# Reordering and rebalancing the convolution branch of a two-layer hybrid encoder on one NeuronCore

## The chip, the cores and the metric

The kernel runs on 1 core of a Trainium2 chip, in one launch. The metric is device microseconds of that core; the time given is the median of three runs. Beside them one execution was taken with the hardware profiler; all views below are of that execution.

## The reference

The input is 512 tokens by 1024 features, float32. Two layers follow one another; each adds half a SwiGLU feed-forward block, then a mixer, then half of a second SwiGLU block, with an RMS norm ahead of each part and one at the end. In the mixer the normed input is projected by `w_in` to 1696 columns: 384 for query latents, 256 for key/value latents, 32 for a rotary key, and 2 x 512 for a convolution branch.

```python
def conv_group(u_raw, conv_w, conv_b, ln_g, ln_b):
    a, g = u_raw[..., :CONV_W], u_raw[..., CONV_W:]
    u = a * jax.nn.sigmoid(g)
    y = lax.conv_general_dilated(u, conv_w[:, None, :], window_strides=(1,),
        padding=[(CONV_K - 1, 0)], feature_group_count=CONV_W, ...)
    y = y + conv_b
    return jax.nn.silu(layer_norm(y, ln_g, ln_b))
...
x = x + 0.5 * swiglu(rms_norm(x, ffn1_norm[l]), ...)
p = rms_norm(x, mix_norm[l]) @ w_in[l]
attn = mla_group(...)          # 8 heads, block-causal, RMS-normed q and k, rotary part
conv = conv_group(p[..., o_cv:], ...)
x = x + jnp.concatenate([attn, conv], axis=-1) @ w_out[l]
x = x + 0.5 * swiglu(rms_norm(x, ffn2_norm[l]), ...)
x = rms_norm(x, post_norm[l])
```

The depthwise convolution is causal and has 31 taps on each of 512 channels.

## The kernel before

Activations lie transposed, 128 features by 512 tokens a tile. Every float32 matrix product is made of three passes in the reduced format (`mm3`, lines 153 to 155): high part times high part, high times low, low times high. So every weight needs a high part, cast by ACT (L137), and a remainder, source minus high part. The remainder is made in one of three ways by `load_w`: a subtraction on DVE, one on POOL (kind "wo"; both L143), or, for kind "sum", ACT writes the negated source rounded to the reduced format (L140) and POOL issues a DMA that adds the source from HBM onto it (L141). High parts and remainders have four buffers each, raw weights three; SyncE issues the raw loads.

The program is written with a tile framework. It knows the data dependencies, and at build time it fixes the order of instructions on each engine by simulating the program with a planner's costs: of what is ready, what comes first in the program goes first. `tc.issue_after(ins)` lets instructions of the block go on their engine only behind `ins`. On the chip each engine then executes its instructions in that order.

The mixer (`mix_body`, once a layer) takes its projections in the order of `SEQ`: query latents, the first two convolution groups, key latents (`latent_k`), their transposes (`kt`, L714), token terms, queries (`uq`), keys (`uk`), and convolution inputs 2 and 3 (`conv_in`). The four convolution groups are 128 channels each; `glu` leaves group c's input in `u[c]`. Then come the eight heads, staged by hand: transposes, scores, softmax, transposed probabilities, values and, for each pair of heads, a split of the output (`turn_out`). The attention output is in `at`.

The convolution stands behind attention in the program, so its instructions fill gaps of the engines while attention runs. `TAPS` gives for each group how many of the 31 taps (the last tap, with the bias, among them) do not go to DVE. Tap products s = 1 to n-1 are made by ACT into one of three buffers `pr` (L931) and added by POOL into `ys[c]` (L933). The other taps are fused multiply-adds on DVE into a PSUM bank `acc` (L927), which ACT begins (L923). Group 2 has all its taps on ACT and POOL, group 3 has all on DVE. POOL's adds of s >= 16, and those of groups past 1, stand behind the last reciprocal root of the keys. A DVE add joins the two parts (L938); three more DVE adds form the sum of the four groups, `ysum` (L941).

The layer norm over 512 channels follows: a matmul with a constant matrix gives the mean (`pm`, L952), DVE subtracts it (L958), ACT squares, DVE adds the squares, PE sums them (L197), POOL takes the reciprocal root (L172), PE spreads it (L216), and scale and SiLU finish each group (L968, L970). Meanwhile PE runs early groups: for output tile m the half of `w_out` that multiplies attention (12 matmuls). `E1`, `E2`, `E3` and `WOG` say how many of them stand ahead of the mean, of the sums, of the spread and of the rest; output tiles are then finished in groups of `WOG`. The temporaries `tmp()` have five buffers that are shared by all of this.

Of the kernel before, what the change touches and what calls it, by code (L numbers as in the profile page):

```python
# [7 lines left out]
FP = mybir.dt.float32  # L8
# [3 lines left out]
AF = mybir.ActivationFunctionType  # L12
ALU = mybir.AluOpType
AX = mybir.AxisListType

P = 128
D = 1024
S = 512
L = 2
KD = D // P  # L20
# [3 lines left out]
DR = 32  # L24
# [3 lines left out]
KVL = 256  # L28
# [5 lines left out]
WC = 1024  # L34
# [3 lines left out]
NP = 3  # L38
NC = 2
CHUNKS = ((0, 2), (2, 5), (5, 8), (8, 11))  # L40
TAPS = (14, 17, 31, 0)
AHEAD = 2
PAUSE = 16
SEQ = "q0 R c1 q1 q2 qo k kt tt uq uk c2 c3"
# [2 lines left out]
GLUP = 0  # L47
EARLY = "s"
PRELOAD = 1
E1 = 0  # L50
E2 = 2
E3 = 3
WOG = 3
WAKE = 10
KS = (0, 2, 4, 6, 1, 3, 5, 7)
WOP = 4
# [17 lines left out]
def encoder_kernel(ctx: ExitStack, tc: tile.TileContext, xT, consts, vecs, rgain, wgu1, wd1, wdq1,  # L74
# [11 lines left out]
    def nm(s):  # L86
        uid[0] += 1
        return f"{s}{uid[0]}"
# [4 lines left out]
    def tmp(w=S, dt=FP):  # L93
        return tmps.tile([P, w], dt, tag="t", name=nm("t"))

    def bank():
        return psum.tile([P, S], FP, tag="ps", name=nm("ps"))

    def tiny(tag, w, dt=FP):
        return small.tile([P, w], dt, tag=tag, name=nm(tag))  # L100

    V, A, G, T = nc.vector, nc.scalar, nc.gpsimd, nc.tensor
# [26 lines left out]
    def vv(l, name):  # L129
        o, w = VOFF[name]  # L130
        return vec[:, l, o:o + w]

    def load_w(src, w, kind=""):
        raw = wpool.tile([P, WC], FP, tag="raw", name=nm("raw"), bufs=3)
        nc.sync.dma_start(out=raw[:, :w], in_=src)
        hi = wpool.tile([P, WC], FR, tag="wh", name=nm("wh"))
        order["cast"] = A.copy(hi[:, :w], raw[:, :w]).ins  # L137
        lo = low()
        if kind == "sum":
            A.activation(lo[:, :w], raw[:, :w], AF.Copy, scale=-1.0)  # L140
            G.dma_start(out=lo[:, :w], in_=src, accum_op=ALU.add)  # L141
            return hi, lo
        (G if kind in POOLW.split() else V).tensor_tensor(lo[:, :w], raw[:, :w], hi[:, :w].bitcast(FP),  # L143
                                                          ALU.subtract)
        return hi, lo

    def low():
        return wpool.tile([P, WC], FR, tag="wl", name=nm("wl"))

    order = {}  # L150

    def mm3(o, lh, ll, rh, rl, first, last, free=False):
        T.matmul(o, lh, rh, start=first, stop=False, skip_group_check=free)  # L153
        T.matmul(o, lh, rl, start=False, stop=False, skip_group_check=free)  # L154
        order["mm"] = T.matmul(o, ll, rh, start=False, stop=last, skip_group_check=free).ins  # L155
        return order["mm"]
# [52 lines left out]
    def spread(r):  # L209

        dg = tmp()
        V.tensor_tensor(dg.rearrange("p (t j) -> p t j", t=NT),
                        ident[:, None, :].to_broadcast([P, NT, P]),
                        r[:, :, None].to_broadcast([P, NT, P]), ALU.mult)
        ps = bank()
        order["spread"] = T.matmul(ps, ones, dg, start=True, stop=True).ins  # L216
        return ps
# [7 lines left out]
    def group(o, w, rhs, ks, n, ts=slice(0, S)):  # L225

        for k in ks:
            c = slice(k * P, (k + 1) * P)
            order["product"] = mm3(o, w[0][:, c], w[1][:, c], rhs[k][0][:, ts], rhs[k][1][:, ts], k == 0, k == n - 1)
# [386 lines left out]
    def mix_body(kpool, l, gx, norm, done):  # L616
        u, order = [], {}

        def kept(dt=FP):
            return kpool.tile([P, S], dt, tag="m", name=nm("m"), bufs=10)  # L620
        ys = [kpool.tile([P, S], FP, tag="y", name=nm("y"), bufs=3) if n else None for n in TAPS]

        def glu(pa, pg):
            tg = tmp()
            V.tensor_tensor(tg, pg, R, ALU.mult)
            sg = tmp()
            order["gate"] = A.activation(sg, tg, AF.Sigmoid).ins
            ta = tmp()
            V.tensor_tensor(ta, pa, R, ALU.mult)
            uc = kept()  # L630
            (G if GLUP else V).tensor_tensor(uc, ta, sg, ALU.mult)
            u.append(uc)

        def conv_in(c):
            pp = []
            for j in range(2):
                ps = bank()
                group(ps, load_w(wcv[l, 2 * c + j], WC, f"c{c}"), gx, range(KD), KD)
                pp.append(ps)
            glu(*pp)  # L640

        gql, gkl = vv(l, "gql"), vv(l, "gkl")
        KW = KVL + DR
        stq = Stats()
        cqT, ckT, pq, scqs, vs = [], [], [], [], []
        ssl, sspe = tiny("ssl", NT), tiny("sspe", NT)
# [18 lines left out]
        def latent_k():  # L665

            pk = [bank() for _ in range(NT)]
            for k0 in range(0, KD, 3):
                n = min(3, KD - k0)
                wh, wl = load_w(wkl[l, :, k0 * KW:(k0 + n) * KW], n * KW, "k")  # L670
                for k in range(k0, k0 + n):
                    cs = slice((k - k0) * KW, (k - k0 + 1) * KW)
                    for t in range(NT):
                        ts_ = slice(t * P, (t + 1) * P)
                        mm3(pk[t][:, :KW], gx[k][0][:, ts_], gx[k][1][:, ts_], wh[:, cs], wl[:, cs],
                            k == 0, k == KD - 1)
            for t in range(NT):
                A.copy(ckl[t // 2][:, t % 2], pk[t][:, :KVL])
                A.copy(cke[:, t], pk[t][:, KVL:KW])
                j = tmp()  # L680
                A.activation(j[:, :KVL], pk[t][:, :KVL], AF.Square, accum_out=ssl[:, t:t + 1])
                j = tmp()
                A.activation(j[:, :DR], pk[t][:, KVL:KW], AF.Square, accum_out=sspe[:, t:t + 1])


        tabs = []
# [73 lines left out]
        def up_kv(w, t, n=S):  # L760

            ts_ = slice(t * P, (t + 1) * P)
            ps = bank()
            for k in range(2):
                cs = slice(k * n, (k + 1) * n)
                mm3(ps, ckT[k][0][:, ts_], ckT[k][1][:, ts_], w[0][:, cs], w[1][:, cs], k == 0, k == 1)
            return ps
# [127 lines left out]
        with tc.issue_after(order["turned"]):  # L895
            for t in range(NT):
                ps = up_kv(wv, t)
# [15 lines left out]
        ysum = None  # L913
        for c, n in enumerate(TAPS):
            tap = lambda k: cw[:, c * CK + k:c * CK + k + 1]
            acc = psum.tile([P, S], FP, tag="cv", name=nm("cv"), bufs=1) if n < CK else None
            first = dict(func=AF.Identity, scale=tap(CK - 1), bias=cb[:, c:c + 1])
            if n:
                A.activation(ys[c], u[c], **first)
            for s in range(n or 1, CK):  # L920
                k = CK - 1 - s
                if s == n:
                    A.activation(acc[:, s:], u[c][:, :S - s], AF.Copy, scale=tap(k))  # L923
                    continue
                if s == 1 and not n:
                    A.activation(acc, u[c], **first)
                V.scalar_tensor_tensor(acc[:, s:], u[c][:, :S - s], tap(k), acc[:, s:], ALU.mult, ALU.add)  # L927
            for s in range(1, n):
                k = CK - 1 - s
                pr = kpool.tile([P, S], FP, tag="pr", name=nm("pr"), bufs=3)  # L930
                A.activation(pr[:, s:], u[c][:, :S - s], AF.Copy, scale=tap(k))  # L931
                with tc.issue_after(order["keys"]) if s >= PAUSE or c > 1 else nullcontext():
                    order["conv"] = G.tensor_tensor(ys[c][:, s:], ys[c][:, s:], pr[:, s:], ALU.add).ins  # L933
            if not n:
                A.copy(u[c], acc)
                ys[c] = u[c]
            elif n < CK:
                V.tensor_tensor(ys[c][:, n:], ys[c][:, n:], acc[:, n:], ALU.add)  # L938
            if c:
                last, ysum = ysum or ys[0], ysum or tmp()  # L940
                V.tensor_tensor(ysum, last, ys[c] if n else acc, ALU.add)  # L941
        early = []

        def early_groups(ms):
            with tc.issue_after(heads[H - 1][EARLY]):
                for m in ms:
                    early.append(bank())
                    group(early[m], wo[m], at, range(4), KD)

        early_groups(range(E1))  # L950
        pm = bank()
        T.matmul(pm, onesm, ysum, start=True, stop=True)  # L952
        if PRELOAD:
            A.activation(tiny("pre", 1), ysum[:, 0:1], AF.Silu)
        early_groups(range(E1, E2))
        st = Stats()
# [5 lines left out]
        pr = spread(r)  # L962
        early_groups(range(E3, WOG))
        lg, lb = vv(l, "lg"), vv(l, "lb")
        cv = []
        for c in range(4):
            z = tmp()
            V.tensor_tensor(z, ys[c], pr, ALU.mult)  # L968
            s = tmp()
# [3 lines left out]
        ac = at + cv  # L973
        for m0 in range(0, KD, WOG):
            ms = range(m0, min(m0 + WOG, KD))
            os = [bank() for _ in ms] if m0 else early
# [77 lines left out]
    gx = []  # L1054
    st = Stats()
    f = gained(0, "g1", gx, first_gain)
# [20 lines left out]
    gx = [gx[KS.index(m)] for m in range(KD)]  # L1077
# [27 lines left out]
    for l in range(L):  # L1105
        nx, st1, done = follow(l, "gm")
        ffn(l, gx, norm, wgu1, wd1, wdq1, vv(l, "g1"), done, w0 if l == 0 else None)
        gx = nx
        nx, st2, done = follow(l, "g2")
        mix(l, gx, Norm(st1), done)  # L1110
        gx = nx
# [3 lines left out]
        if l + 1 < L:  # L1115
# [10 lines left out]
            gx = nx  # L1126
# [118 lines left out]
```

## Time and profile before

| what | value |
|---|---|
| median of 3 runs | 1814.83 us (1812.89 to 1814.99) |
| profiled execution, its own time | 1811.83 us |
| its span, first to last instruction | 1810.0 us |
| mean granted TensorE clock | 0.994 |
| PE / DVE / ACT / POOL busy | 1777.9 / 1502.8 / 1099.6 / 411.9 us |

Times of views are in microseconds from the span's start. A row of a timeline gives start, length, engine, line, operation, the tiles written and read, shape, count, and in brackets how long the engine had stood idle before it and what ended that. A row of the waits gives the total, the number of times and the longest. A row for one source line gives least, median and greatest length in nanoseconds. Buffer numbers are left out of names, so that `t` is any temporary and `ps` any PSUM bank. A matmul's length overlaps with the next one's; the spacing of starts is the pace.

### The profile page before, as it was taken

What the parts mean: (1) busy time and instruction counts of PE and PEld (TensorE: products, weight loads), DVE (VectorE), ACT (ScalarE), POOL (GpSimd) and SP (SyncE); (2) the same over time, 40 slices, a digit from 0 to 9 for tenths busy, and PEclk for the clock granted to TensorE, in tenths of its full rate; (3) what the DMA queues carried; (4) which work ended last, traced back from release to release, by engine and by line L of the source; (5) the groups of instructions that cost most, each with busy time, mean ns of one, the idle gap of its engine ahead of it and who ended that gap; (6) DMA issues with size and microseconds to landing.
All of it is one profiled execution on the core that took longest, in us unless ns stands there. A gap on an engine that the chain in (4) does not pass through costs nothing. (4 is left out here: it accounts for less than half of the span.)

```text
span 1810.0 us, 29098 instructions
## 1 busy us (share of the span) xinstructions
PE 1777.9 (98%) x11238; PEld 1585.2 (88%) x11238; DVE 1502.8 (83%) x2271; ACT 1099.6 (61%) x1729; POOL 411.9 (23%) x335
## 2 busy tenths in 40 slices
PE   9999999999999999999999999999999999999998
PEld 7899999888668899999888999998886788999997
DVE  7898988679956989898779989876899669989884
ACT  5565656477953575756645657554778535656564
POOL 1000000278714000000320000002876320000102
PEclk9999999999999999999999999999999999999999
DMA  4657574324203466665426575743250126575642
GB/s 169 174 124 184 130 186 112 108 84 118 51 12 111 117 161 160 154 162 135 122 65 169 121 193 119 194 112 110 80 130 23 37 86 169 132 180 135 178 120 73
DMA packets 70411, 226.14 MB, mean 125 GB/s; under 512 B 7936, under 2 KB 8320, under 8 KB 70272
## 3 DMA queue, kind: packets, MB, share of 16 engines
q1 hardware_dynamic: 54000, 169.74, 29.5%
q0 software_dynamic: 16128, 54.53, 17.6%
q8 instruction: 88, 1.44, 0.3%
q14 instruction: 51, 0.42, 0.1%
q10 hardware_dynamic: 144, 0.00, 0.0%
HBM read 222.15 MB, written 2.10 MB: 124 GB/s over the span
## 5 line engine op out<-in xcount | busy, mean ns | idle before, releaser
L154 PE MATMUL ps<-r,wh 128*128 128x256 f32 (+1 forms) x2556 | 812.5, 318 | 0.0
L153 PE MATMUL ps<-r,wh 128*128 128x256 f32 (+1 forms) x2556 | 809.2, 320 | 2.3 <-ACT wh L1064 1.3
L155 PE MATMUL ps<-r,wl 128*128 128x256 f32 (+1 forms) x2364 | 756.7, 322 | 1.8 <-DVE wl L245 1.6
L153 PEld LDWEIGHTS ps<-r,wh 128*128 128x128 f32 x2556 | 483.8, 189 | 45.0 <-ACT wh L137 3.4
L154 PEld LDWEIGHTS ps<-r,wh 128*128 128x128 f32 x2556 | 484.6, 190 | 34.9 <-issue 1.4
L155 PEld LDWEIGHTS ps<-r,wl 128*128 128x128 f32 x2364 | 448.3, 190 | 37.8 <-DVE wl L245 3.4
L372 PE MATMUL ps<-xj,wh 128*128 128x512 f32 x864 | 304.8, 392 | 4.6 <-DVE t L425 4.6
L137 ACT CAST wh<-raw 128x1024 fp32r<-128x1024 f32 (+3 forms) x148 | 130.8, 891 | 190.7 <-PE ps L154 93.1
L389 POOL DMA_DIRECT2D ls<-in_wgu x72 | 62.5, 869 | 734.3 <-ACT ls L388 604.7
L243 ACT CAST wh<-fr 128x1024 fp32r<-128x1024 f32 (+1 forms) x160 | 157.8, 986 | 111.3 <-DVE fr L409 47.8
L143 DVE TENSOR_TENSOR wl<-raw,wh 128x1024 fp32r<-128x1024 f32 (+3 forms) x132 | 147.0, 1122 | 84.1 <-ACT wh L137 83.5
L245 DVE TENSOR_TENSOR wl<-fr,wh 128x1024 fp32r<-128x1024 f32 (+1 forms) x160 | 182.3, 1139 | 20.5 <-ACT wh L243 20.5
L372 PEld LDWEIGHTS ps<-xj,wh 128*128 128x128 f32 x864 | 161.3, 188 | 36.3 <-DVE t L425 6.3
L933 POOL TENSOR_TENSOR y<-y,pr 128x511 f32<-128x511 f32 (+29 forms) x118 | 160.9, 1368 | 32.6 <-ACT pr L931 26.4
L373 PE MATMUL ps<-xj,ls 128*128 128x256 f32 x576 | 161.3, 280 | 0.0
L245 DVE TENSOR_TENSOR wl<-raw,wh 128x1024 fp32r<-128x1024 f32 (+1 forms) x100 | 113.5, 1136 | 14.8 <-ACT wh L243 14.3
L243 ACT CAST wh<-raw 128x1024 fp32r<-128x1024 f32 (+1 forms) x100 | 98.1, 981 | 44.8 <-PE ps L154 27.7
L190 POOL TENSOR_TENSOR r<-r,t 128x512 f32<-128x512 f32 x45 | 76.5, 1709 | 175.6 <-ACT t L186 174.8
L373 PEld LDWEIGHTS ps<-xj,ls 128*128 128x128 f32 x576 | 108.3, 188 | 0.2
L388 ACT ACTIVATE ls<-fr 128x1024 fp32r<-128x1024 f32 (+1 forms) x56 | 56.1, 1001 | 85.6 <-PE ps L373 49.6
L931 ACT ACTIVATE pr<-m,vec 128x511 f32<-128x511 f32 (+29 forms) x118 | 85.7, 738 | 15.4 <-POOL y L933 15.0
L927 DVE SCALAR_TENSOR_TENSOR cv<-m,vec,cv 128x493 f32<-128x493 f32 (+29 forms) x118 | 85.8, 727 | 4.2 <-ACT cv L923 2.9
(243 smaller groups left out, 2869.2 us busy)
## 6 DMA issues: line engine op xcount, KB each, us to landing
fr<-in_wgu SPq DMA_DIRECT2D x112, 512.0 KB, 4.1
ls<-in_wgu POOLq DMA_DIRECT2D x72, 512.0 KB, 5.9
raw<-in_wgu SPq DMA_DIRECT2D x62, 512.0 KB, 5.1
fr<-in_wdq SPq DMA_DIRECT2D x48, 384.0 KB, 5.4
ls<-in_wdq POOLq DMA_DIRECT2D x32, 384.0 KB, 4.7
raw<-in_wd SPq DMA_DIRECT2D x32, 384.0 KB, 3.1
raw<-in_wd SPq DMA_DIRECT2D x32, 256.0 KB, 2.7
raw<-in_wcv SPq DMA_DIRECT2D x16, 512.0 KB, 3.6
```

The costliest lines, as they stand in the source:

```text
L137: order["cast"] = A.copy(hi[:, :w], raw[:, :w]).ins
L143: (G if kind in POOLW.split() else V).tensor_tensor(lo[:, :w], raw[:, :w], hi[:, :w].bitcast(FP), ALU.subtract)
L153: T.matmul(o, lh, rh, start=first, stop=False, skip_group_check=free)
L154: T.matmul(o, lh, rl, start=False, stop=False, skip_group_check=free)
L155: order["mm"] = T.matmul(o, ll, rh, start=False, stop=last, skip_group_check=free).ins
L243: A.copy(hi[:, :w], src[:, :w])
L245: order["lo"] = V.tensor_tensor(lo[:, :w], src[:, :w], hi[:, :w].bitcast(FP), ALU.subtract).ins
L372: T.matmul(o, w[0][:, c], both, start=start and k == 0, stop=False, skip_group_check=True)
L373: last = T.matmul(o[:, 0:HS], w[1][:, c], both[:, 0:HS], start=False, stop=k == 3, skip_group_check=True).ins
L927: V.scalar_tensor_tensor(acc[:, s:], u[c][:, :S - s], tap(k), acc[:, s:], ALU.mult, ALU.add)
L931: A.activation(pr[:, s:], u[c][:, :S - s], AF.Copy, scale=tap(k))
L933: order["conv"] = G.tensor_tensor(ys[c][:, s:], ys[c][:, s:], pr[:, s:], ALU.add).ins
```

## The change

It makes five edits, all in the mixer and so once a layer.

1. ACT's products s >= 5 of groups 1, 2 and 3 stand, in ACT's order, behind the last square of the key latents (`order["latent"]`, L683).
2. Group 3 gets five taps off DVE: one starting activation on ACT, four products on ACT with four adds on POOL, and a joining add on DVE. The DVE taps go from 30 to 25. Tiles of tag `y` are now taken group by group; group 3 takes the buffer that group 0 leaves, because group 0's joined result now goes into `u[0]` (its first 14 columns by an ACT copy).
3. `ysum` is kept in `u[1]`, the input of group 1, in place of a temporary.
4. The four weight tiles of convolution inputs 2 and 3 are loaded as kind "sum": the remainder leaves DVE for an ACT copy and a POOL-issued DMA.
5. `E1` goes from 0 to 1 and `WOG` from 3 to 4: one early group stands ahead of the mean, one of four behind the spread, and output tiles are finished in two groups of four.

```diff
-TAPS = (14, 17, 31, 0)
+TAPS = (14, 17, 31, 5)
+HELD = 5
...
-E1 = 0
+E1 = 1
 E2 = 2
 E3 = 3
-WOG = 3
+WOG = 4
...
-        ys = [kpool.tile([P, S], FP, tag="y", name=nm("y"), bufs=3) if n else None for n in TAPS]
+        ys = []
...
-                group(ps, load_w(wcv[l, 2 * c + j], WC, f"c{c}"), gx, range(KD), KD)
+                group(ps, load_w(wcv[l, 2 * c + j], WC, "sum" if c > 1 else "c1"), gx, range(KD), KD)
...
-                A.activation(j[:, :DR], pk[t][:, KVL:KW], AF.Square, accum_out=sspe[:, t:t + 1])
+                order["latent"] = A.activation(j[:, :DR], pk[t][:, KVL:KW], AF.Square,
+                                               accum_out=sspe[:, t:t + 1]).ins
...
+            ys.append(kpool.tile([P, S], FP, tag="y", name=nm("y"), bufs=3) if n else None)
...
-                A.activation(pr[:, s:], u[c][:, :S - s], AF.Copy, scale=tap(k))
+                with tc.issue_after(order["latent"]) if c and s >= HELD else nullcontext():
+                    A.activation(pr[:, s:], u[c][:, :S - s], AF.Copy, scale=tap(k))
...
-                V.tensor_tensor(ys[c][:, n:], ys[c][:, n:], acc[:, n:], ALU.add)
+                y = ys[c]
+                if c == 0:
+                    ys[c] = u[c]
+                    A.copy(ys[c][:, :n], y[:, :n])
+                V.tensor_tensor(ys[c][:, n:], y[:, n:], acc[:, n:], ALU.add)
             if c:
-                last, ysum = ysum or ys[0], ysum or tmp()
+                last, ysum = ysum or ys[0], u[1]
                 V.tensor_tensor(ysum, last, ys[c] if n else acc, ALU.add)
```

## The prediction

> **What bounds the kernel now.** I read the page first, then what PE waits for, then a table of stretches through the first mixer (L0, about 320 to 560 us) with the matching stretches of the second (L1).
>
> ```profile
> span 1810.0 us, 29098 instructions
> PE 1777.9 (98%) x11238; PEld 1585.2 (88%) x11238; DVE 1502.8 (83%) x2271; ACT 1099.6 (61%) x1729; POOL 411.9 (23%) x335
> PE ps L952 <- DVE t L941: 6.9, 2, 3.5
> PE ps L714 <- ACT r L678: 4.3, 2, 2.2
> 401.60:403.70 2.10, 0.00 (x0) 0.00 (x0) 1.90 (x3) 2.10 (x6) 2.02 (x2) 1.00 0.08 33
> 403.70:410.50 6.80, 6.79 (x26) 6.70 (x27) 6.73 (x15) 6.80 (x30) 6.00 (x7) 0.51 0.27 77
> 426.70:448.50 21.80, 21.80 (x98) 17.98 (x97) 21.80 (x38) 11.79 (x17) 18.65 (x16) 1.00 0.59 166
> 456.70:508.40 51.70, 50.16 (x353) 33.09 (x352) 48.31 (x95) 43.86 (x111) 30.91 (x25) 1.00 0.11 26
> 511.90:516.50 4.60, 4.60 (x12) 3.34 (x13) 3.38 (x6) 2.60 (x5) 0.00 (x0) 0.63 0.00 0
> 1301.40:1308.20 6.80, 6.80 (x26) 6.70 (x27) 6.73 (x15) 6.80 (x30) 5.92 (x6) 0.51 0.28 80
> 1409.20:1425.00 15.80, 15.62 (x67) 12.00 (x68) 8.98 (x15) 6.44 (x11) 1.03 (x1) 1.00 0.00 1
> ```
>
> In a stretch's row stand its length, then the busy time of PE, weight loads, DVE, ACT and POOL, then the granted clock. PE is busy 98% of the span, and the change removes no matmul, so only two things can be won: the 32 us in which PE stands idle, and stretches where it runs at a low clock. The two longest waits are both in the mixer, once a layer. The first, on the key-latent copies (L678), is followed in both layers by 6.8 us at clock 0.51. The second, on the group sums (L941), is followed in L0 by 4.6 us at 0.63 and in L1 by none. Between them PE is full (21.80 of 21.80) or nearly so (50.16 of 51.70), though DVE is nearly full too.
>
> **The latent copies held first.**
>
> ```profile
> 398.22 0.71 ACT L931 ACTIVATE pr<-m,vec 128x507 f32<-128x507 f32 x1
> 401.34 0.72 ACT L931 ACTIVATE pr<-m,vec 128x506 f32<-128x506 f32 x1 [2.41 <-POOL y L933]
> 401.96 0.82 ACT L137 CAST wh<-raw 128x768 fp32r<-128x768 f32 x1
> 402.68 0.71 ACT L931 ACTIVATE pr<-m,vec 128x505 f32<-128x505 f32 x1
> 403.30 0.35 ACT L678 COPY r<-ps 128x256 f32<-128x256 f32 x1
> 401.27 0.29 PE L155 MATMUL ps<-wh,r 128*128 128x288 f32 x1
> 403.71 0.62 PE L714 MATMUL ps<-cst,r 128*128 128x128 f32 x2 [2.14 <-ACT r L678]
> 450.23 0.32 PE L815 MATMUL ps<-cst,kn 128*96 128x128 f32 x1 [0.83 <-DVE kn L784]
> ```
>
> PE ends the key latents at 401.56, but ACT stands 2.41 us before product s=6 of group 1, which waits for POOL to free one of three product buffers; the cast and s=7 follow, and only then the copy. ACT executes in order, so the copy pays for POOL. Products s=5, 6 and 7 of group 1 are those now put behind the last latent square. ACT is then free from 398.9, the cast can go there, and the first copy costs about 0.35 plus a hand-over: I leave 0.45 us of the wait. Won per layer: 1.7 of idle, and (1 - 0.51) x 6.8 = 3.3 of lost clock if the gap is then too short to lower it; after the 0.83 us gap at 450 the clock stayed at 1.00 (stretch from 456.70). Both layers: 10.0 us. Bounds: 0, if another wait as long takes its place, to 4.3 + 6.7 = 11.0. Behind the held products queue only POOL's adds of group 1, costed below.
>
> **The end of attention.**
>
> ```profile
> 506.50 1.89 PE L876 MATMUL ps<-r,m 128*64 128x512 f32 x14
> 511.86 0.70 PE L952 MATMUL ps<-t,onesm 128*128 128x512 f32 x1 [3.46 <-DVE t L941]
> 508.52 0.69 DVE L879 TENSOR_TENSOR t<-ps,t 128x512 f32<-128x512 f32 x1 [1.65 <-PE ps L876]
> 509.12 0.68 DVE L941 TENSOR_TENSOR t<-y,y 128x512 f32<-128x512 f32 x1
> 511.12 0.68 DVE L941 TENSOR_TENSOR t<-t,cv 128x512 f32<-128x512 f32 x1
> 1409.23 1.12 PE L952 MATMUL ps<-t,onesm 128*128 128x512 f32 x2 [3.46 <-DVE t L941]
> 1423.31 1.19 PE L153 MATMUL ps<-r,wh 128*128 128x512 f32 x4
> 482.09 9.43 POOL L933 TENSOR_TENSOR y<-y,pr 128x488 f32<-128x488 f32 x7 [0.44 <-ACT pr L931]
> 427.39 0.39 PE L154 MATMUL ps<-r,wh 128*128 128x512 f32 x1
> 427.62 0.39 PE L155 MATMUL ps<-r,wl 128*128 128x512 f32 x1
> ```
>
> POOL's last group add ends at 491.5, yet the first of the three sums starts at 509.12, right behind the last reader of attention's temporaries (L879), after DVE stood idle 1.65 us. I read that as a wait for one of the five temporaries, not for data. In the freed u[1] the sums need none. The mean (L952) can then start when PE leaves the last values at 508.4, or after the nine matmuls of early group 0 whose operands exist, 9 x 0.23 = 2.1 us later (0.23 is the spacing of the two rows at 427). From the mean to the first convolution product L1 took 1423.31 - 1409.23 = 14.1 us, with PE busy nearly throughout; early groups 0 to 3 are that work, and they ran before too, so a fourth early group by itself adds nothing. Won per layer: 3.46 with the mean at once, 1.4 with it 2.1 later; I take 2.8, as the mean may also slip in earlier. L0 gets (1 - 0.63) x 4.6 = 1.7 more, for its clock. Both: 7.3; bounds 2.8 to 8.6.
>
> **Taps, remainders and queues.**
>
> ```profile
> L927 DVE SCALAR_TENSOR_TENSOR cv<-m,vec,cv x118: 685/728/755, 373.2 to 1398.1; 128x494 f32<-128x494 f32 x6, 128x493 f32<-128x493 f32 x6, 128x492 f32<-128x492 f32 x6, 128x491 f32<-128x491 f32 x6
> L931 ACT ACTIVATE pr<-m,vec x118: 700/722/852, 373.1 to 1386.1; 128x511 f32<-128x511 f32 x6, 128x510 f32<-128x510 f32 x6, 128x509 f32<-128x509 f32 x6, 128x508 f32<-128x508 f32 x6
> L933 POOL TENSOR_TENSOR y<-y,pr x118: 1207/1268/2105, 373.9 to 1387.7; 128x511 f32<-128x511 f32 x6, 128x510 f32<-128x510 f32 x6, 128x509 f32<-128x509 f32 x6, 128x508 f32<-128x508 f32 x6
> L938 DVE TENSOR_TENSOR y<-y,cv x4: 656/666/675, 396.9 to 1344.1; 128x498 f32<-128x498 f32 x2, 128x495 f32<-128x495 f32 x2
> 425.52 2.35 DVE L143 TENSOR_TENSOR wl<-raw,wh 128x1024 fp32r<-128x1024 f32 x2
> L140 ACT ACTIVATE wl<-raw x8: 1042/1052/1059, 438.5 to 1354.4; 128x1024 fp32r<-128x1024 f32 x8
> L141 POOL DMA_DIRECT2D wl<-in_wout x8: 870/890/1147, 444.3 to 1355.7; - x8
> DMA to landing us min/median/max: 5.1/6.4/8.7
> 420.62 2.00 ACT L137 CAST wh<-raw 128x1024 fp32r<-128x1024 f32 x2
> ```
>
> Per layer DVE loses five taps, 5 x 0.73 = 3.6, gains one add of 0.67, and loses four remainders of 1.18, 4.7: 7.7 less. ACT gains 4 x 0.72 of products and 4 x 1.05 of negated copies, 7.1 in all; its 14-column copy is small, and the other starting activations replace two of the old form. POOL gains 4 x 1.27 of adds and 4 x 0.89 of issues, 8.6. On POOL they push the last add from 491.5 to about 500, plus up to 5 for the hold; the sums are wanted at 508.4, so this is hidden. Without that cover each us past 508 is a us of PE. ACT's four products come after group 2's and lie where ACT stood idle behind 490.
>
> PE gets from the lighter DVE at most the 0.83 at the keys (L0 alone) and the 1.54 us a layer that it idles inside attention, 3.9 in all; below, 0. I take 1.8, since most of those gaps inside attention end at ACT.
>
> The new path of a remainder is on PE's path. Queries free the buffer for group 2's first weights at 420.6; the cast ends at 421.6, the negated copy at 422.65 at best, and only then POOL issues. With the median landing of 6.4 the remainder is there at 429.05; PE uses it at 427.62. With a 0.4 hand-over PE waits 1.8 us per layer, 3.6 in all. DVE's subtraction was done in time. Best: landing 5.1 and no hand-over, 0.1 a layer; worst: an add of 1.27 ahead and 8.7, 5.0 a layer. The other three have 5.5 us of PE work (24 matmuls) more each, so I put them at 0.
> [...]
>
> Output groups in fours want their last two weights about 5 us earlier, prepared by POOL: 0.5 a layer, 1.0 in all, bounds 0 to 4, by the two early matmul groups (5.5) that hid them.
>
> Sum: -10.0 - 7.3 - 1.8 + 3.6 + 1.0 = -14.5 us. The profiled execution took 1811.83 (span 1810.0 and 1.83 around it), 3.00 under the median of 1814.83. So 1797.3 for a like execution, 1800.3 for the median. All best: -11.0 - 8.6 - 3.9 + 0.2 = -23.3, 1791.5.
>
> **Rivals.** *The remainder's path becomes the new stall (slower).* If the first remainder of group 2 waits behind POOL's adds and reciprocal roots and lands late, PE idles over 2 us there and, as behind the latents, loses 3.3 more to the clock. The gains make 19.1 us for both layers, less 1.0: the point is a wait of 18.1 / 2 - 3.3 = 5.8 us a layer. At 8 us it costs 2 x 11.3 = 22.6 against 18.1: +4.5, 1819. For it: POOL is 18.65 of 21.80 busy there and DVE 21.80; against: the worst of my bounds is 5.0.
> [...] The eight issues of 0.87 to 1.15 us show no long one, though none ran at the queries.
>
> *The tail gains little.* The order on each engine is fixed at build time; if early group 0, complete with its last operand, stands before the mean, the mean starts near 511 as now, PE idles behind the four groups instead, and the end of attention gives 2.8 or less: with a landing wait of 3 (and its clock in one layer) -14.5 + 4.5 + 2.4 + 3.3 = -4.3, 1810.5.
>
> *The hold does nothing.* PE may wait at the same place for the cast or for another copy: -14.5 + 10.0 = -4.5, and with a landing wait of 3 a layer -2.1, 1812.7.
>
> **How the numbers follow.** A difference of 0.2%, 3.6 us, is about what measurement can tell from none. Forecast 0.56, tail 0.16, hold 0.08, remainder stall 0.20. The likeliest gives 1800.3, its own range 1792 to 1808. Faster takes the forecast and the tail, 0.72; same 0.08; slower 0.20. The range runs from 1791 to 1817, which leaves out the worse half of the slow rival and little below.
>
> **What would show it.** Right: the wait of L714 on L678 under 0.6 us and clock 1.00 behind it; L941 well ahead of the last L879; L952 within 2.5 us of the last L876; a wait of PE on the remainder's landing of 1 to 3 us once a layer; POOL's last group add before the last values. Wrong: a gap over 2 us before group 2's products with a low clock behind it, or L952 still waiting over 3 us.

## The result and the profile after

The changed kernel takes 1825.34 us (median of 4 runs, 1824.19 to 1825.70) against 1814.91 for the kernel before: 1.0058 times as long, interval 1.0041 to 1.0075. The forecast was 1800.3. The profiled execution took 1825.7 us, with a span of 1823.9. In the code after, lines lie a little further down: the transfer of a remainder is issued at L142, the reciprocal root is L173, a product L935, a POOL add L937, the mean L960.

The page and the waits of PE after:

```profile
PE 1779.7 (98%) x11238; PEld 1581.8 (87%) x11238; DVE 1500.1 (82%) x2255; ACT 1116.4 (61%) x1751; POOL 425.3 (23%) x351
PE ps L156 <- DMA wl<-in_wcv: 17.3, 2, 9.0
PE ps L835 <- ACT r L841: 4.5, 7, 1.1
PE ps L154 <- ACT r L161: 2.8, 2, 1.4
PE ps L154 <- ACT wh L138: 2.1, 3, 1.0
```

Both waits that the prediction wanted gone are gone: neither the key-latent copies nor the group sums are in the list. In their place stands a larger one, 17.3 us in two waits, for the remainder of convolution input 2.

To see where the time went I cut each mixer at four matmuls: the last of the key latents, the first of the scores, the last set of row sums, the first convolution product. The rows are the first mixer's stretches from latents to the last query and from there to the scores, before and then after (length, busy PE, weight loads, DVE, ACT, POOL, clock):

```profile
401.30:421.10 19.80, 17.66 (x91) 17.27 (x90) 19.32 (x36) 18.58 (x53) 18.49 (x17) 0.83 0.21 61
421.10:456.70 35.60, 34.77 (x162) 28.80 (x161) 35.21 (x57) 25.56 (x38) 31.25 (x24) 1.00 0.60 157
456.70:505.20 48.50, 46.96 (x323) 31.21 (x322) 47.14 (x93) 42.33 (x109) 30.91 (x25) 1.00 0.12 27
```

```profile
401.60:416.00 14.40, 14.40 (x91) 14.24 (x90) 14.13 (x28) 11.59 (x38) 9.71 (x11) 1.00 0.28 87
416.00:462.80 46.80, 36.82 (x163) 29.66 (x162) 40.66 (x61) 33.73 (x52) 39.90 (x33) 0.89 0.70 166
462.80:513.30 50.50, 47.05 (x323) 31.18 (x321) 46.28 (x90) 48.57 (x118) 38.20 (x31) 1.00 0.12 25
```

The hold did what it was to do: 14.40 us in place of 19.80, PE full, clock 1.00. The next stretch then grew by 11.2 us, with 10 us of PE idle. The third row is attention, 2 us longer, with ACT busy 48.57 of 50.50 where it had been 42.33 of 48.50. The table gives both layers of all kernels, from the starts of those matmuls.

| kernel | median us | latents to scores | scores to last row sums | to first convolution product |
|---|---|---|---|---|
| before | 1814.9 | 55.5 / 54.4 | 48.4 / 49.1 | 22.4 / 20.8 |
| after | 1825.3 | 61.1 / 61.5 | 50.5 / 50.8 | 20.0 / 20.0 |
| after, remainders on DVE (e1) | 1825.4 | 58.2 / 60.3 | 53.0 / 52.7 | 20.0 / 20.0 |
| remainders alone (e2) | 1825.5 | 61.4 / 61.5 | 48.5 / 48.5 | 22.8 / 22.4 |
| after, first remainder on DVE (e3) | 1828.5 | 62.2 / 57.0 | 53.9 / 52.8 | 20.0 / 20.0 |
| hold alone (e4) | 1824.0 | 56.7 / 60.3 | 49.6 / 48.2 | 22.4 / 20.8 |
| after, issue first (e6) | 1810.7 | 51.8 / 53.1 | 50.6 / 50.1 | 22.0 / 22.6 |
| four product buffers (e7) | 1825.1 | 59.9 / 59.6 | 48.5 / 48.5 | 22.4 / 22.4 |
| hold, fewer taps (e8) | 1819.1 | 55.2 / 59.7 | 49.6 / 48.2 | 22.4 / 22.1 |
| sums alone (e9) | 1812.0 | 54.4 / 54.4 | 50.4 / 49.2 | 21.7 / 22.2 |
| hold, adds behind keys (e11) | 1813.1 | 50.5 / 50.1 | 50.8 / 50.8 | 24.6 / 24.6 |
| the same with remainders (e12) | 1805.8 | 51.1 / 49.9 | 50.2 / 49.3 | 23.2 / 22.9 |
| hold, remainders, issue first (e13) | 1811.0 | 51.3 / 53.5 | 50.2 / 49.9 | 20.8 / 22.4 |
| after, adds behind keys (e14) | 1805.8 | 49.4 / 51.2 | 50.6 / 50.0 | 20.5 / 22.1 |
| e12, fewer adds (e15) | 1843.3 | 51.3 / 49.4 | 48.4 / 47.5 | 43.1 / 43.1 |
| remainders, adds behind keys (e16) | 1813.9 | 56.5 / 54.5 | 49.3 / 49.3 | 24.0 / 21.3 |

Where PE loses it, in the timelines of PE, ACT and POOL after:

```profile
423.85 0.40 PE L155 MATMUL ps<-r,wh 128*128 128x512 f32 x1
433.20 0.80 PE L156 MATMUL ps<-r,wl 128*128 128x512 f32 x1 [8.95 <-DMA wl<-in_wcv]
433.80 0.63 PE L154 MATMUL ps<-r,wh 128*128 128x512 f32 x1
418.53 1.14 ACT L141 ACTIVATE wl<-raw 128x1024 fp32r<-128x1024 f32 x1
407.42 0.60 POOL L692 TENSOR_TENSOR tab<-cst,rg 128x64 f32<-128x64 f32 x2 [4.37 <-DVE wkl L727]
417.96 3.31 POOL L937 TENSOR_TENSOR y<-y,pr 128x503 f32<-128x503 f32 x2
421.77 1.65 POOL L173 TENSOR_TENSOR scq<-ssh,minus_half 128x8 f32<-128x8 f32 x1 [0.51 <-DVE ssh L751]
423.39 1.26 POOL L937 TENSOR_TENSOR y<-y,pr 128x501 f32<-128x501 f32 x1
424.59 0.90 POOL L142 DMA_DIRECT2D wl<-in_wcv  x1
DMA to landing us min/median/max: 5.5/8.0/11.1
```

ACT had the negated copy ready at 419.67. POOL issued the transfer only at 424.59: ahead of it in POOL's order stood two held adds, a root that itself had to wait, and one more add. It landed when PE started, 433.2. The row at 407.42 shows the other side: POOL now idles 4.37 us right behind the latents, where before it was busy with six adds of group 1, four of which are now held:

```profile
400.03 8.57 POOL L933 TENSOR_TENSOR y<-y,pr 128x509 f32<-128x509 f32 x6
409.16 0.60 POOL L690 TENSOR_TENSOR tab<-cst,rg 128x64 f32<-128x64 f32 x2 [0.57 <-DVE wkl L725]
```

So the hold moved these four adds out of a hole in POOL's time into the stretch where POOL makes the roots of queries and keys and issues the remainders.

### The profile page after: what moved, and what is told of

Read it like the earlier page. It is cut to its first block, busy times and chain, and to the rows that moved or that the text cites. A ratio compares the mean times of both kernels' runs of the same rounds, so it can differ in the third digit from the quotient of the medians.

```text
span 1823.9 us, 29142 instructions
## 1 busy us (share of the span) xinstructions
PE 1779.7 (98%) x11238; PEld 1581.8 (87%) x11238; DVE 1500.1 (82%) x2255; ACT 1116.4 (61%) x1751; POOL 425.3 (23%) x351
## 5 line engine op out<-in xcount | busy, mean ns | idle before, releaser
L156 PE MATMUL ps<-r,wl 128*128 128x256 f32 (+1 forms) x2364 | 758.2, 322 | 19.2 <-DMA wl<-in_wcv 17.3
L154 PEld LDWEIGHTS ps<-r,wh 128*128 128x128 f32 x2556 | 484.4, 190 | 49.5 <-ACT wh L138 5.9
L244 ACT CAST wh<-fr 128x1024 fp32r<-128x1024 f32 (+1 forms) x160 | 157.8, 986 | 107.7 <-DVE fr L410 51.2
L144 DVE TENSOR_TENSOR wl<-raw,wh 128x1024 fp32r<-128x1024 f32 (+4 forms) x124 | 136.4, 1108 | 88.0 <-ACT wh L138 87.4
L937 POOL TENSOR_TENSOR y<-y,pr 128x511 f32<-128x511 f32 (+28 forms) x126 | 172.9, 1378 | 35.6 <-ACT pr L935 29.8
L191 POOL TENSOR_TENSOR r<-r,t 128x512 f32<-128x512 f32 x45 | 74.2, 1657 | 177.0 <-ACT t L187 176.4
L389 ACT ACTIVATE ls<-fr 128x1024 fp32r<-128x1024 f32 (+1 forms) x56 | 56.1, 1001 | 88.9 <-PE ps L374 49.5
L935 ACT ACTIVATE pr<-m,vec 128x511 f32<-128x511 f32 (+29 forms) x126 | 91.6, 752 | 14.5 <-POOL y L937 14.0
L390 POOL DMA_DIRECT2D ls<-in_wdq x32 | 27.7, 865 | 271.6 <-ACT ls L389 261.4
```

Source lines behind the costliest of these rows:

```text
L244: A.copy(hi[:, :w], src[:, :w])
L390: G.dma_start(out=lo[:, :n], in_=w, accum_op=ALU.add)
```

## The experiments

### Is it the remainder's path?

The first theory was the prediction's own rival: the remainders' new path is the whole loss.

Run e1, the kernel after with all remainders back on DVE:

```diff
-                group(ps, load_w(wcv[l, 2 * c + j], WC, "sum" if c > 1 else "c1"), gx, range(KD), KD)
+                group(ps, load_w(wcv[l, 2 * c + j], WC, "c1"), gx, range(KD), KD)
```

> The changed kernel with the remainders of convolution inputs 2 and 3 back on DVE; the other four edits stay. Theory A, the remainder's path is the whole loss: the stretch from the last query matmul to the first head transpose, 39.6 and 38.2 us in the changed kernel against 27.4 before, goes back to about 27.4, which takes 12.1 + 10.8 = 22.9 us off 1825.3: about 1802, faster than before by 12. Rival B, the four subtractions (4.7 us a layer) make DVE the bound at the keys and at the heads: 1807 to 1812. Rival C, the stall comes from the held products and not from the remainders: it stays, about 1822.

Run e2, the kernel before with the remainders alone:

```diff
-                group(ps, load_w(wcv[l, 2 * c + j], WC, f"c{c}"), gx, range(KD), KD)
+                group(ps, load_w(wcv[l, 2 * c + j], WC, "sum" if c > 1 else "c1"), gx, range(KD), KD)
```

> The kernel before with one edit alone: the remainders of convolution inputs 2 and 3 by ACT's negated copy and a POOL-issued transfer. Theory A, the path itself is too long (negated copy, POOL's queue, landing of 8 us): PE waits 4 us or more a layer before the first remainder and its clock drops, +12 to +22 us, 1827 to 1837. Rival C, only the products held behind the latents, with their adds, stand ahead of the negated copy and of the issue: without the hold the wait is under 2 us a layer, 1815 to 1819.

Run e3, after with only the first of the four back on DVE (`"sum" if c > 2 or c == 2 and j else "c1"`):

> The changed kernel with only the first weight tile of convolution input 2 back on DVE; the other three remainders stay on the new path. Theory A as predicted, with 5.5 us of matmuls for each further tile as cover: no wait is left, 1802 as with all four on DVE, or 2 to 3 below it for the 3.5 us a layer that DVE is spared. Rival D, the second tile takes the wait over, since it landed 2.7 us behind the first and gets only 5.5 us of cover from a first that was 10.8 late: a wait of 5 us a layer with a low clock, 1812 to 1818.

Run e4, before with the hold alone:

```diff
+HELD = 5
...
+                order["latent"] = A.activation(j[:, :DR], pk[t][:, KVL:KW], AF.Square, ...).ins
...
+                with tc.issue_after(order["latent"]) if c and s >= HELD else nullcontext():
                     A.activation(pr[:, s:], u[c][:, :S - s], AF.Copy, scale=tap(k))
```

> The kernel before with one edit alone: products s >= 5 of groups 1 to 3 behind the last latent square on ACT. Theory A: the 2.14 us wait and the 6.8 us at clock 0.51 go, as in the changed kernel, where the stretch from the last latent matmul to the last query matmul shrank by 5.45 and 4.33 us: -9.8, 1805. Rival: the later adds on POOL delay the keys' roots or the group sums and give half of it back, 1810.

Measured against 1814.99 for the kernel before, timed beside them (in brackets the ratio and its 95% interval): e1 1825.43 (1.0063, 1.0046 to 1.0080), e2 1825.51 (1.0060, 1.0040 to 1.0081), e3 1828.45 (1.0079, 1.0060 to 1.0099), e4 1823.97 (1.0058, 1.0037 to 1.0079). The theory fell. e1 shows it: without the remainders' path the loss is the same. e3 missed both its forecasts: PE waits 4.8 us in two for the first tile's subtraction on DVE and 7.0 us in two for a transfer. And the hold alone, which I had counted as the largest gain, is 9 us slower than before. In e4 PE waits for DVE, at a remainder and at the scaled keys, and POOL's last root of the keys ends at 446.88, 44.7 us behind the last latent product, against 444.35 and 43.1 before (PE and POOL in e4, then POOL before):

```profile
426.30 0.50 PE L156 MATMUL ps<-r,wl 128*128 128x512 f32 x1 [2.86 <-DVE wl L144]
452.36 0.31 PE L817 MATMUL ps<-cst,kn 128*96 128x128 f32 x1 [2.52 <-DVE kn L786]
439.20 7.68 POOL L173 TENSOR_TENSOR sck<-ssk,minus_half 128x8 f32<-128x8 f32 x4
```

```profile
436.42 7.93 POOL L172 TENSOR_TENSOR sck<-ssk,minus_half 128x8 f32<-128x8 f32 x4 [1.68 <-DVE ssk L777]
```

In e2 there is no hold, and yet PE waits 13.8 us for the remainder in the two layers. So two edits lose 9.0 and 10.5 us, each by itself, and together (10.4) no more than the larger.

### POOL's order, or DVE's load?

That left theory D, DVE is full from the latents to the scores and whatever PE gains is given back there; and theories P and Q, POOL's group adds, standing ahead of a root (P) or of a remainder's issue (Q), are what is late.

Run e6, the kernel after with the adds of group 1 (s >= 5) behind the issue of the first remainder:

```diff
-                with tc.issue_after(order["keys"]) if s >= PAUSE or c > 1 else nullcontext():
+                behind = "keys" if s >= PAUSE or c > 1 else "first" if c and s >= HELD else None
+                with tc.issue_after(order[behind]) if behind else nullcontext():
                     order["conv"] = G.tensor_tensor(ys[c][:, s:], ys[c][:, s:], pr[:, s:], ALU.add).ins
```

> The kernel after, with POOL's adds of products s>=5 of group 1 put behind the issue of convolution input 2's first remainder, so that POOL issues it as soon as ACT's negated copy is there. Theory Q (the 4.9 us that POOL let the transfer stand are most of its lateness): the wait on the remainder falls from 17.3 us to about 7.5, last query to first head transpose from 39.5/38.2 to about 33, time 1814 to 1817. Theory L (the landing of 8 us beside other loads sets it): wait stays over 13, time 1822 to 1826. Theory D (VectorE's row of work from the latents to the keys is the bound by now): the wait on the remainder falls, but a wait for the scaled keys (kn) of over 2 us a layer comes in its place and last query to first scores stays at 43 or more; time 1820 to 1824.

Run e7, the kernel before with four product buffers:

```diff
-                pr = kpool.tile([P, S], FP, tag="pr", name=nm("pr"), bufs=3)
+                pr = kpool.tile([P, S], FP, tag="pr", name=nm("pr"), bufs=4)
```

> The kernel before with four product buffers in place of three, nothing held: ACT then need not stand 2.4 us before a product, so the key-latent copies can come early, while POOL's adds of group 1 stay where they were. Theory D (VectorE is full from the latents to the first scores, 48 of 50 us): the latents' wait of 2.1 shrinks, and what is won there (up to 5 us a layer) is handed back as waits on VectorE before the first scores; last latent to first scores stays within 2 us of before (55.5/54.4), time 1812 to 1817. Theory P (in the held kernel it was the adds displaced among the reciprocal roots that cost): without displacement the gain stays, last latent to first scores falls by 4 to 5, time 1804 to 1808.

Run e8, the hold alone with six DVE taps of group 1 left out:

```diff
+                if c == 1 and s >= CK - 6:
+                    continue
```

> Before with the hold alone, and with 6 of VectorE's 14 taps of group 1 left out (they are not computed): 4.3 us less of VectorE's work a layer between the latents and the first scores, POOL and ACT as in the hold alone (1823.97). Theory D: last query to first scores falls from 42.4/44.8 by 4 or more a layer, waits for kn and for the remainders under 2 us each, time 1812 to 1817. Theory P (POOL's displaced adds alone): these waits stay, time 1821 to 1825.

Measured against 1813.50: e6 1810.66 (0.9984, 0.9975 to 0.9994), e7 1825.08 (1.0069, 1.0052 to 1.0086), e8 1819.09 (1.0034, 1.0021 to 1.0047). e6 decides for Q and goes past its lower end: one condition on POOL's adds turns 10.4 us slower into 2.8 faster. The wait on the remainder is 4.7 us in two, no wait for keys takes its place, and latents to scores fell by 9.3 and 8.4. e8 speaks against D: 4.3 us less of DVE's own work a layer took only 1.5 and 0.6 us off latents to scores; its time, 1819.09, lies between the two ranges. e7 missed both theories, since the copies came no earlier (PE still waits 4.3 us for them), but it points to P another way: with a buffer more, ACT runs further ahead and seven adds stand before the roots where six had stood, the last root of the keys ends 45.5 us behind the latents in place of 43.1, and PE waits 8.0 us for the keys (POOL and PE's waits in e7):

```profile
401.73 9.94 POOL L933 TENSOR_TENSOR y<-y,pr 128x509 f32<-128x509 f32 x7
439.25 9.16 POOL L172 TENSOR_TENSOR sck<-ssk,minus_half 128x8 f32<-128x8 f32 x4
PE ps L815 <- DVE kn L784: 8.0, 2, 4.3
PE ps L714 <- ACT r L678: 4.3, 2, 2.2
```

Run e11, the hold alone with those adds behind the last root of the keys, and run e12, the same with the remainders on the new path:

```diff
-                with tc.issue_after(order["keys"]) if s >= PAUSE or c > 1 else nullcontext():
+                with tc.issue_after(order["keys"]) if s >= (HELD if c else PAUSE) or c > 1 else nullcontext():
```

> Before with the hold, as in the run with the hold alone (1823.97), and POOL's adds of the held products of group 1 put behind the last reciprocal root of the keys: the roots and position factors on POOL have nothing of group 1 ahead of them from the latents on; remainders on VectorE, taps and the end of attention as before. Theory P (a held add that stands before a root delays what VectorE does next, and that is what the hold costs): last latent to first scores falls from 56.7/60.3 with the hold alone to 50 to 53, 2 to 5 below before's 55.5/54.4; time 1804 to 1809. Theory D (VectorE's own work between the latents and the first scores, 48 of 50 us, is the bound whatever POOL does): last latent to first scores stays at 54 to 57, time 1812 to 1816. Rival: POOL's adds, now later, end behind the last values and the sums come late; then pairs' end to the first convolution product grows over 24.

> The same kernel with the four remainders of convolution inputs 2 and 3 on the new path (negated copy, accumulating transfer). Theory P with VectorE next: the remainders take 4.7 us off VectorE, PE waits 2 to 3 us a layer for the first remainder (4.7 in both with the adds behind its issue), last latent to first scores 50 to 53, about as in its pair; time within 3 of it. Theory Q (the new path is itself dear, beyond the queue on POOL): over 4 us slower than its pair.

Run e14, the kernel after with the same line changed, and run e16, e2 with it (5 in place of `HELD`, no hold):

> The whole change as it is, with one edit: POOL's adds of the held products of group 1 (s>=5) stand behind the last reciprocal root of the keys. Theory P (where these adds stand on POOL is what made the change slow): last latent to first scores falls from 61.1/61.5 to 50 to 52, the wait on the remainders from 17.3 to under 5, time 1806 to 1812. Theory Q2 (taps, sums or groups of four cost by themselves): over 1815. If the adds, all late now, end behind the last values, the end of attention (20.0 with the adds early) grows to 23 or more.

> Before with the remainders alone on the new path (1825.51 with POOL's adds where they fell), and with POOL's adds of products s>=5 of group 1 behind the last root of the keys; no hold, so ACT still stands before a product ahead of the latent copies. Theory P: the wait on the remainders falls from 13.8 to under 5, last query to first head transpose from 36.0/37.1 to 28 to 30, time 1809 to 1814, between before and the same with the hold (1805.75). Theory L (the transfer itself is too slow): wait over 10, time over 1819.

Measured: e11 1813.06 (0.9989, 0.9980 to 0.9999) and e12 1805.75 (0.9944, 0.9926 to 0.9963) against 1814.41; e14 1805.79 (0.9960, 0.9948 to 0.9973) and e16 1813.88 (0.9993, 0.9981 to 1.0005) against 1814.71. e12 beat its pair by 7.3 us where I had expected at most 3. One condition turns the whole change from 10.4 us slower to 8.9 us faster than before. In e14 nothing of group 1 stands ahead of a root from the latents on (POOL, then PE's waits, then the stretch from the last query to the scores):

```profile
414.16 1.64 POOL L173 TENSOR_TENSOR scq<-ssh,minus_half 128x8 f32<-128x8 f32 x1 [3.56 <-DVE ssh L751]
416.69 0.92 POOL L142 DMA_DIRECT2D wl<-in_wcv  x1 [0.90 <-ACT wl L141]
428.06 7.47 POOL L173 TENSOR_TENSOR sck<-ssk,minus_half 128x8 f32<-128x8 f32 x4
435.50 1.37 POOL L937 TENSOR_TENSOR y<-y,pr 128x507 f32<-128x507 f32 x1
PE ps L156 <- DMA wl<-in_wcv: 1.7, 2, 1.0
PE ps L198 <- DVE r L191: 3.6, 2, 1.8
PE ps L835 <- ACT r L841: 4.3, 8, 1.0
415.60:450.70 35.10, 35.10 (x163) 28.75 (x162) 29.00 (x55) 27.90 (x40) 31.76 (x28) 1.00 0.87 209
```

The roots end at 435.53, 34.2 us behind the latents, and PE is full for all 35.10 us of this first layer. e11's time lies in theory D's range, but its latents to scores fell as theory P has it. What took the rest is the price of the late adds, but not as the rival had it: POOL's last add ends at 504.28, before the first group sum at 507.70. By the trace, group 1's join comes at 462.84 in place of 450.09, only then is the PSUM accumulator free for group 3, and six of group 3's taps run on DVE behind 500 us in place of one. The mean starts 1.2 us later behind the row sums than before, and attention is 2 us longer; why the way on from the mean also grew, by 0.9 and 2.8 us, stays open. e16 shows the new path without hold and without queue: its wait is 2.9 us in place of 13.8, and the time is that of before.

One thing these runs do not separate. An add that stands among the roots also runs beside DVE's work, and in these runs DVE then took longer for the same instructions: 1512.2 us in e4 against 1495.4 in e11. The rows are DVE's busy time in e4 and in e11 (the kernel before has 1502.8 for the same 2271 instructions), then in e14 (the kernel after has 1500.1 for the same 2255), then one line of the rotary step that the queries' scaling follows, in the kernel after and in e14:

```profile
PE 1778.2 (98%) x11238; PEld 1582.5 (87%) x11238; DVE 1512.2 (83%) x2271; ACT 1100.1 (60%) x1729; POOL 415.5 (23%) x335
PE 1779.7 (98%) x11238; PEld 1585.2 (87%) x11238; DVE 1495.4 (83%) x2271; ACT 1099.0 (61%) x1729; POOL 419.1 (23%) x335
PE 1776.1 (99%) x11238; PEld 1580.5 (88%) x11238; DVE 1485.0 (82%) x2255; ACT 1111.0 (62%) x1747; POOL 425.1 (24%) x351
L710 DVE TENSOR_TENSOR q<-t x4: 413/2303/3178, 420.1 to 1331.6; 128x256 f32<-128x256 f32 x4
L710 DVE TENSOR_TENSOR q<-t x4: 414/420/426, 418.2 to 1315.7; 128x256 f32<-128x256 f32 x4
```

Of the slow ones in the kernel after, the one at 420.05 took 1.50 us beside the second of POOL's two adds of the row at 417.96; the two longest, 3.18 us at 429.99 and 3.11 at 1331.58, ran beside an add and other work of POOL. So an add among the roots may cost in two ways: POOL gets to the root or the issue later, and DVE gets later to what the root needs. For the first remainder the first way is read off above, 4.9 us in POOL's order, of which 0.51 is a wait of POOL for DVE. Without the hold the second way is small: e2 and e16 have 1489.6 and 1485.2 us of DVE for the same 2263 instructions, 4.4 apart, and 11.6 us of time between them. In the whole change the condition removes both ways at once, and how much of its 19.5 us is due to each stays open.

### What the rest of the change is worth

Run e9, before with the sums in the freed buffers, one early group before the mean, and SiLU's table loaded behind the last exponential:

```diff
-E1 = 0
+E1 = 1
...
+                    ys[c] = u[c]
...
-                last, ysum = ysum or ys[0], ysum or tmp()
+                last, ysum = ysum or ys[0], u[1]
...
+            with tc.issue_after(heads[H - 1]["exp"]):
                 A.activation(tiny("pre", 1), ysum[:, 0:1], AF.Silu)
```

> Before with the edits at the end of attention alone (group 0's sum in u[0], running group sum in u[1], one early group of output products before the mean; taps, hold, remainders and groups of three as before), and with the early load of Silu's table put behind the last exponential. Theory T (the freed buffer does remove the wait, and the tables that were loaded three times in place of once gave half of it back): wait for the sums (3.5 a layer) gone, last row sum to first convolution product from 22.4/20.8 to about 18.5 in both, attention as before, time 1806 to 1811. Rival U (attention's own 2 us of extra length in the changed kernel come from the sums' early adds on VectorE): scores to last row sum 2 us longer, time 1812 to 1815.

Run e13, e6 without the five taps of group 3, the sums and the output groups of four:

> The kernel with the adds behind the first remainder's issue (1810.66), without the five more taps of group 3 off VectorE, without the sums in the freed buffers and with three early groups of output products, none before the mean, as before. It tells what those edits cost together. If the sums and the taps make attention longer by the 1 to 2 us that scores to the last row sum grew by (50.6/50.1 against 48.4/49.2), and gain nothing at the end: 1806 to 1809. If they are worth the 7.3 of the forecast: 1815 to 1819.

Run e15, e12 with four products of group 2 back on DVE (`TAPS = (14, 17, 27, 0)`):

> The best kernel so far (hold, remainders on the new path, adds behind the keys; 1805.75) with four products of group 2 given back to VectorE as taps (27 in place of 31): some 5 us less of POOL's adds and 2.9 of ACT a layer, 3.6 us more on VectorE. If POOL's late last add is what the end of attention pays (23.2/22.9 against 22.4/20.8 before): last row sum to first convolution product back to 20.8 to 22.4, time 1801 to 1804. If VectorE is the next bound inside attention: scores to last row sum over 51, time 1806 to 1811.

Measured: e9 1812.04 (0.9991, 0.9982 to 1.0000) against 1813.50; e13 1810.97 (0.9979, 0.9966 to 0.9991) against 1814.41; e15 1843.31 (1.0160, 1.0144 to 1.0175) against 1814.71. e9 missed theory T: the wait for the sums is gone and the stretch behind the last row sums is no shorter in sum (43.9 against 43.2). Its time is at the lower end of rival U's range, but attention grew by 2.0 us in the first layer and by 0.1 in the second. e13 fell between its two forecasts; against e6 (1810.66), taps, sums and groups of four are together worth nothing either way. e15 tells nothing about POOL's last add. Groups 2 and 3 then use the one PSUM accumulator in turn, so that 24 of group 3's taps on DVE run behind attention, at 508.04 in one row, and PE waits for them:

```profile
508.04 18.48 DVE L929 SCALAR_TENSOR_TENSOR cv<-m,vec,cv 128x505 f32<-128x505 f32 x24
PE ps L955 <- DVE t L944: 46.6, 2, 23.3
```

## Why the prediction was wrong

**The hold.** Forecast -10.0 for both layers together; from the last latent to the last query it gave 5.4 and 4.3, with the clock at 1.00. This term was right.

**What stands behind the hold: the step that failed.** I wrote that POOL's adds queue behind the held products and costed them as load, 8.6 us a layer and up to 5 for the hold, "hidden" by the slack between 491.5 and 508.4. That asked only when POOL ends. It did not ask what stands behind each moved add in POOL's order. That slack was there (POOL's last add ends at 505.56, before the mean at 516.64) and did not help. What was lost were the 4.37 us behind the latents, in which POOL now idles, and what was delayed were the roots and the issue: 11.1 and 11.4 us a layer from the last query to the scores. e4 shows it without the remainders, e2 without the hold, and e14 undoes it with one condition. Nor did I ask what an add slows beside it: by my sum DVE was to be 15.4 us less busy (7.7 a layer), and it was 2.7 less (1502.8 to 1500.1), against 17.8 less in e14.

**The first remainder.** Forecast 1.8 us a layer, bounds 0.1 to 5.0; measured 8.95 and 8.30. In the first layer the parts are: POOL's hand-over 4.9 in place of 0.4, as above; the landing 8.6 in place of 6.4; and 0.4 since PE wanted it 3.4 us earlier (424.25) while the copy was ready only 3.0 earlier (419.67). With the 1.8 that makes 8.9. My worst bound let one add of 1.27 stand ahead; it was two adds, a root and an add. The slower rival had this mechanism, with the point of decision at 5.8 us a layer, and gave 1819 at 8 us; I gave it 0.20. Freed of the queue the wait is 0.9 us a layer in e14: for a POOL that is free the sign was right, and the size lies within my bounds at half the forecast.
The sixteen landings of the changed kernel took 5.5 to 11.1 us, median 8.0; the eight before it had taken 5.1 to 8.7, median 6.4.

**The end of attention.** Forecast -7.3; the stretch gave 2.3 and 0.8, and in e9 and e14 nothing worth naming in sum. My reading of the wait was right: with the sums in `u[1]` the second sum runs at 501.57, ahead of attention's last product on DVE (L881, 520.10). But I took the 14.1 us from mean to product as work of PE that would follow an earlier mean. It is a chain through DVE, ACT and POOL that PE's early groups merely fill: after the change the mean comes 3.3 us earlier relative to the row sums, and the way from it to the product is 16.7 us in both layers. Where early groups run ahead of the mean, PE waits inside the chain instead; L198 on L191 in e14, 1.8 us a layer, is such a wait. In the changed kernel the chain also holds a table load of ACT. SiLU's early load now stands ahead of the last exponential, so that ACT loads three tables at the end of attention where it had loaded one, at 509.88:

```profile
508.70 1.28 ACT L962 ACT_TABLE_LOAD   x1
510.22 1.28 ACT L841 ACT_TABLE_LOAD   x1
529.94 1.28 ACT L978 ACT_TABLE_LOAD   x1 [7.97 <-DVE t L976]
```

e14 has the load once, and 13.9 and 15.5 us from mean to product.

**The lighter DVE.** Forecast -1.8; attention became 2.1 and 1.7 longer. I put ACT's products "where ACT stood idle" and did not bound them above. In the stretch ACT is now 96% busy, and PE's wait for its probabilities (L835 on L841) is 4.5 us in seven, where before it was 2.2 in six (L833 on L839). But ACT's load is not shown to be the cause. e13 takes the four products out of e6, with the sums and the groups of four: ACT is then busy 46.9 and 47.0 us of the stretch in place of 49.8 and 49.5, and attention is only 0.4 and 0.2 us shorter. The cause stays open.

**Output groups in fours.** Forecast +1.0; the stretch from the first product to the next norm's sums is 44.3 to 44.4 us before and after.

The terms add up: -9.8 to the last query, +22.5 from there to the scores, +3.8 in attention, -3.1 behind it, +0.1 are 13.5 of the 13.9 us between the two spans. With POOL's order mended (e14) the forecast of 1800.3 is still missed by 5.5 us. From the latents to the scores e14 gains more than I had summed up there; what is missing is in attention and behind it, and how much of either could be had stays open.

## What to carry to other kernels

An instruction that is moved back on an in-order engine moves what it feeds. Find where that lands on the next engine, and list what stands behind it there, not just whether that engine has time left at the end. Where a queue serves both bulk work and short steps that others wait for, hold the bulk behind the last short step; here that one condition was worth 19.5 us. It has a price where something waits for the bulk itself, as group 3 did for the accumulator in e11. And before moving filler out of a stretch, ask whether the stretch is a chain that needed it.

## What the runs showed of the hardware

POOL's roots of the queries took longer in a run where DVE subtracted remainders beside them. In e11 two roots took 6.49 us together from 419.17, and three subtractions of 1.21 us started meanwhile on DVE, at 419.60, 421.60 and 425.41. In e12 the four subtractions a layer of inputs 2 and 3 are gone, and the same two roots took 3.28 us from 419.58 (for all query roots minimum, median and longest, in ns, first e11 and then e12):

```profile
L173 POOL TENSOR_TENSOR scq<-ssh,minus_half x8: 1637/2092/4888, 414.5 to 1326.1; 128x8 f32<-128x8 f32 x8
```

```profile
L173 POOL TENSOR_TENSOR scq<-ssh,minus_half x8: 1632/1650/2362, 414.9 to 1320.3; 128x8 f32<-128x8 f32 x8
```

No run separates the subtractions from the rest of DVE's work: in e12 a root of 2.31 us at 426.08 had none beside it. The longer roots are not where e12 gains its 7.3 us on e11: from latents to scores, where these roots run, e12 takes 51.1 and 49.9 us and e11 50.5 and 50.1.

How long the clock stays low did not grow with the gap before it. Before the change a gap of 2.14 us was followed by 6.8 us at 0.51; after it, behind 8.95 and 8.30 us, matmuls started 0.43 us apart in place of 0.23 (granted clock 0.52 and 0.50) for 3 and 4.5 us only, in the first layer from the row at 433.20 to 436.23 and in the second, from 1335.94, up to these rows:

```profile
1340.37 0.51 PE L154 MATMUL ps<-r,wh 128*128 128x512 f32 x1
1340.71 0.40 PE L155 MATMUL ps<-r,wh 128*128 128x512 f32 x1
```

What sets how long it stays low, these runs do not show.
